# A fp32 transformer layer on one core: a reordered opening, and two modulation-row steps set between two weights

## The chip, the cores and the metric

The kernel runs on one core of a Trainium2 chip. The metric is the device time of one execution in microseconds. Engines are named as the profile names them: PE (TensorE, matrix products), PEld (its weight loads), ACT (ScalarE), DVE (VectorE), POOL (GpSimd), SP (SyncE, which issues nearly all DMA transfers; "SPq" is its queue).

## The reference

One layer on x of 512 tokens x 1024, with a conditioning vector c. All data are fp32.

```python
mod = silu(c) @ w_ada + b_ada            # 9 rows of 1024: sh1 sc1 g1 sh2 sc2 g2 sh3 sc3 g3
u = rms_norm(x, ffn1_norm_g) * (1 + sc1) + sh1
x = x + 0.5 * g1 * swiglu(u, ffn1_w_in, ffn1_w_out)     # a, b = split(u @ w_in); silu(a) * b; @ w_out
u = rms_norm(x, mix_norm_g) * (1 + sc2) + sh2
z = u @ w_mix + b_mix
...
x = x + g2 * (merged @ w_out)            # mLSTM branch and forgetting-attention branch
u = rms_norm(x, ffn2_norm_g) * (1 + sc3) + sh3
x = x + 0.5 * g3 * swiglu(u, ffn2_w_in, ffn2_w_out)
```

The change touches only the first FFN's first half, `u @ ffn1_w_in` (1024 x 5632, that is 22 pairs of 128 columns, a_j and b_j), and the rows of `mod`.

## The kernel before, in words

**Products.** An fp32 product is made of three reduced-precision ones: each operand is split into a high part (`uh`, `wh`) and a rest (`ul`, `wl`), and `mm3` (L106 to L110) adds uh by wh (L108), uh by wl (L109 or L110, as the operands are named) and ul by wh in one PSUM bank. A weight block of 128 x 1024 comes through a ring of three buffers `raw` (L76 to L80, the DMA is issued in L79 by SP), is rounded to `wh` by ACT (L89), and its rest `wl` is made by DVE (L91). A buffer of the ring comes free when its `wl` is made, or, for a piece of w_ada, when DVE has added it; SP's queue goes in order, so a load that waits for a buffer holds up every load behind it.

**The opening, `start`.** It loads x, sums its squares, makes the reciprocal roots in two chains (`chain`, on DVE), scales x by them (`norm`, L616 on ACT, one of them on DVE) and transposes the scaled x into columns (`turn`, L625, PE), four transposes for each of the eight blocks of 128 of D. The modulation of block 0, its shift and its scale, is made on PE: `mod0(v)` (L636) is eight matmuls of the pieces of w_ada with silu(c), v = 0 for the shift, v = 1 for the scale, into columns 128 to 255 and 256 to 383 of one PSUM bank, `cb` (t_207 in the rows below). For the blocks 1 to 7 DVE adds up the pieces (L641, L646, `ac`), and `sums` (L661) folds them on PE into two columns of `cb`. `u_hi` (L663 to L669, ACT) then makes the two columns `m` (L665 shift, L666 scale), `uh` and the unrounded `uf`; `u_lo` (L671, DVE) makes `ul`. Block k is 18 matmuls (L720): three products for each of six PSUM banks, the first three column pairs of the FFN. Inside block k stand the transposes for block k + 1 (at i = 7), and from k = 1 on the sums for it too (at i = 12). In block 0 those sums stand behind the 18 matmuls, behind four transposes of the identity that nobody reads (`fill(4)`, L620). All this is pinned: it is issued in the order in which it is written.

**The rest of the columns, `ffn_in`.** For j = 3 to 21: weight a_j, its 24 matmuls, a call `mid` if there is one, weight b_j, 24 matmuls, then `ffn_h` (silu on ACT L318, product `sl` on DVE L319, `hh` L320, `hl` L321), then `extra(j)`. Here `extra` makes steps of the modulation rows v = 2 to 6 (`ada_row`): step k loads a 128 x 1024 piece through the same ring `raw` and adds it up on DVE (L275 for k = 0, L277 after); step 7 also folds the sum, finishes the row with two matmuls (L289), adds the bias (L290) and stores it to `mod_d` (L291). That is 40 steps; 19 columns with two steps each make 38, and a third step is made at j = 7 and at j = 15. The accumulator `acc` and the bias row `br` share two buffers, so a row's first step waits until the row before is stored.

Of the kernel before, what the change touches and what calls it, by code (L numbers as in the profile page):

```python
# [11 lines left out]
F32 = mybir.dt.float32  # L12
F32R = mybir.dt.float32r
I32 = mybir.dt.int32
AF = mybir.ActivationFunctionType
# [5 lines left out]
P = 128  # L21
T = 512
NT = 4
# [4 lines left out]
NJ0 = 3  # L28
# [18 lines left out]
class Layer:  # L47
# [279 lines left out]
    def ffn_in(self, w_in, j0, hp, tp, extra=None, mid=None):  # L327
        for j in range(j0, NJ):
            pa, pb = self.gbank(), self.gbank()
            self.gemm_stat(pa, self.w_stat(w_in, j * P), 0, T)  # L330
            if mid:
                mid()
            self.gemm_stat(pb, self.w_stat(w_in, FF + j * P), 0, T)
            self.ffn_act(pa, pb, j, 0, T, hp, tp)
            self.lo_after = None
            if extra:
                extra(j)
# [249 lines left out]
    def start(self, st, tp):  # L587

        nc, A, sp, cp = self.nc, self.A, self.sp, self.cp
        w_in = A["ffn1_w_in"][0]  # L590
        w_ada = A["w_ada"][0]
        pin = self.tc.keep_in_program_order
# [11 lines left out]
        def chain(hf):  # L604
            v = sp.tile([P, 2], F32, name=self.nm("v"), tag="v", bufs=2)
            s2 = self.ss[:, 2 * hf:2 * hf + 2, :]
            pin(nc.vector.tensor_scalar(v, s2[:, :, 0], 1.0 / D, EPS, op0=MUL, op1=ADD))
            pin(nc.vector.scalar_tensor_tensor(v, s2[:, :, 1], 1.0 / D, v, op0=MUL, op1=ADD))
            return self.rsqrt(v, 2, pin)
        def norm(tb, h, dve=False):  # L610
            t = xn[tb, h] = st.tile([P, 512], F32, name=self.nm("xn"), tag="xs", bufs=8)
            r = rs[tb // 2][:, tb % 2:tb % 2 + 1]
            if dve:
                pin(nc.vector.tensor_scalar(t, self.x[tb][h], r, None, op0=MUL))
            else:
                pin(nc.scalar.activation(t, self.x[tb][h], AF.Copy, scale=r))  # L616
        def fill(n):

            for i in range(n):
                pin(nc.tensor.transpose(cb[:, 384:512], self.ident, self.ident))  # L620
        def turn(k, tbs):
            if k not in bt:
                bt[k] = self.tbank()
            for tb in tbs:
                pin(nc.tensor.transpose(bt[k][:, tb * P:(tb + 1) * P], xn[tb, k // 4][:, k % 4 * P:(k % 4 + 1) * P], self.ident))  # L625
        def ada_load(k):

            ars[k] = st.tile([P, NK, 2, P], F32, name=self.nm("ar"), tag="ar", bufs=7)
            halves = [(v, i) for v in range(2) for i in (0, 4)] if k == 0 else [(v, i) for i in (0, 4) for v in range(2)]
            for v, i in halves:  # L630
                nc.sync.dma_start(ars[k][:, i:i + 4, v, :], w_ada[i * P:(i + 4) * P, v * D + k * P:v * D + (k + 1) * P]
                                  .rearrange("(i p) n -> p i n", p=P))
        def mod0(v):

            for i in range(NK):
                pin(nc.tensor.matmul(cb[:, 128 * (v + 1):128 * (v + 2)], ars[0][:, i, v, :], self.ccol[:, i:i + 1].to_broadcast([P, P]),  # L636
                                     start=i == 0, stop=i == NK - 1))
# [10 lines left out]
        def load(k):  # L648
            raws[k] = self.raw(sh, [(lambda t, i=i: t[:, i, :],
                                     w_in[k * P:(k + 1) * P, i * FF:i * FF + NJ0 * P]) for i in range(2)])  # L650
# [8 lines left out]
        def sums(k):  # L659
            for v in range(2):  # L660
                pin(nc.tensor.matmul(cb[:, 2 * k + v:2 * k + v + 1], accs[k][:, v, :], self.one, start=True, stop=True))  # L661
        def u_hi(k):
            m = sp.tile([P, 2], F32, name=self.nm("m"), tag="m", bufs=4)  # L663
            c = (cb[:, 2 * k:2 * k + 1], cb[:, 2 * k + 1:2 * k + 2]) if k else (cb[:, 128:129], cb[:, 256:257])
            pin(nc.scalar.activation(m[:, 0:1], c[0], AF.Identity, bias=self.colC[:, 16 + k:17 + k]))  # L665
            pin(nc.scalar.activation(m[:, 1:2], c[1], AF.Identity, scale=self.colC[:, 8 + k:9 + k], bias=self.colC[:, 24 + k:25 + k]))  # L666
            pin(nc.scalar.activation(self.uh[k], bt[k], AF.Identity, scale=m[:, 1:2], bias=m[:, 0:1]))
            ufs[k] = self.tmp(tp, "uf")
            self.last_uf = pin(nc.scalar.activation(ufs[k], bt[k], AF.Identity, scale=m[:, 1:2], bias=m[:, 0:1]))  # L669
# [10 lines left out]
        cb = self.tbank()  # L680
# [8 lines left out]
        norm(1, 0)  # L689
        rs.append(chain(1))  # L690
        norm(2, 0, True)
        norm(3, 0)
        mod0(0)
        turn(0, (0, 1))
        turn(1, (0, 1))
        mod0(1)
        turn(0, (2, 3))
        w_hi(0)
# [9 lines left out]
        for k in range(NK):  # L708
            n = k + 1
            if k + 3 < NK:  # L710
                ada_load(k + 3)
                load(k + 3)
            wh, wl = ws[k]
            for i, (p, b) in enumerate((p, b) for p in range(3) for b in range(2 * NJ0)):
                if n < NK and i == 7:
                    turn(n, range(NT) if k else (2, 3))
                if n < NK and k and i == 12:
                    sums(n)
                s = slice(b // 2 * P, (b // 2 + 1) * P)
                pin(nc.tensor.matmul(acc_ps[b], (wl if p == 1 else wh)[:, b % 2, s], self.ul[k] if p == 2 else self.uh[k],  # L720
                                     start=k == 0 and p == 0, stop=k == NK - 1 and p == 2))
            if n < NK:
                if k == 0:
                    fill(4)
                    sums(n)
                u_hi(n)
                if k < 2:
                    norm(2 * k, 1)
                    norm(2 * k + 1, 1)
                if n + 1 < NK:  # L730
                    mod(n + 1, 1, 6)
                u_lo(n)
                if n + 1 < NK:
                    mod(n + 1, 6, 8)
                    w_hi(n + 1)
                    if n + 2 < NK:
                        mod_first(n + 2)
                    w_lo(n + 1)
# [423 lines left out]
    def run(self):  # L1162
        nc, tc, A = self.nc, self.tc, self.A
# [7 lines left out]
        with tc.tile_pool(name="f1t", bufs=1) as tp:  # L1171
            self.consts(tp)
            with tc.tile_pool(name="st", bufs=1) as st:
                acc_ps = self.start(st, tp)
            with tc.tile_pool(name="f1h", bufs=1) as hp:
                self.h_tiles(hp)
                for j in range(NJ0):
                    self.ffn_h(acc_ps[2 * j], acc_ps[2 * j + 1], j, 0, T, hp, tp)
                ada = (s for v in (2, 3, 4, 5, 6) for s in self.ada_row(v, tp, self.gbank))
                def extra(j):  # L1180
                    next(ada, None)
                    next(ada, None)
                    if j % 8 == 7:
                        next(ada, None)
                self.ffn_in(A["ffn1_w_in"][0], NJ0, hp, tp, extra)
                for _ in ada:
                    pass
                lhs = lambda k: (self.hh[k], self.hl[k])
                self.ss_tile()
                for half in range(2):  # L1190
                    bank = self.tbank if half else self.gbank
                    ada = self.ada_row(7 + half, tp, bank)
                    extra = lambda: next(ada, None)
                    self.token_gemm(lhs, NJ, A["ffn1_w_out"][0], half, self.residual(0.5, 2, half, tp), 2 + half, extra,
                                    (lambda: self.norm_half(0, tp, G2, sh2)) if half else None)
                    for _ in ada:
                        pass
                    if half == 0:
                        G2, sh2 = self.mod_cols(3, gain(R_N2))
            self.norm_half(1, tp, G2, sh2)  # L1200
            for tb in range(NT):
                for h in range(2):
                    nc.sync.dma_start(self.x_d[tb * P:(tb + 1) * P, h * 512:(h + 1) * 512], self.x[tb][h])
            for k in range(NK):
                self.dump(f"u2_{k}", self.uh[k].bitcast(F32))
# [24 lines left out]
        with tc.tile_pool(name="att", bufs=1) as ip:  # L1230
# [35 lines left out]
            for n in range(18):  # L1266
                if n % 4 == 0 and n < 16:
                    advance(fill, 99)
                    g = n // 4
                    fill = with_gates(self.fox_qkv(g + 1, ip), 4 if g else 2) if g < 3 else (s for m in range(NK) for s in self.y_a(m, yp, ip))  # L1270
# [56 lines left out]
        with tc.tile_pool(name="f2t", bufs=1) as tp, tc.tile_pool(name="f2h", bufs=1) as hp:  # L1327
# [5 lines left out]
            step = lambda *_: next(pw, None)  # L1333
# [34 lines left out]
```

## Time and profile before

| | |
|---|---|
| device time, 3 runs | 1344.37, 1344.70, 1345.14 us (median 1344.70) |
| the profiled execution's own time | 1344.62 us |
| its span | 1342.8 us |
| granted TensorE clock, mean | 1.00 |
| PE busy | 1325.6 us, 99% of the span |
| DVE / ACT / POOL busy | 66% / 44% / 3% |
| chain that ended last | PE 91%, DVE 5%, ACT 2%, DMA 1% |

The span is the time from the first to the last instruction that the profiler records; the 1.8 us between it and the execution's time lie around it and are not touched by the change. All rows below count from the span's start. A timeline row gives the start, the duration, engine, line, operation, the tile written and the tiles read, the size, the count of such instructions in a row, and in brackets the idle time before it and what ended that.

### The profile page before, as it was taken

The page shows a single profiled execution, that of the slowest core. Times are in us where ns is not written, and L with a number is a line of the kernel's source. Part 1 is how long each engine was busy: PE and PEld are TensorE (multiplying, and loading weights), DVE is VectorE, ACT ScalarE, POOL GpSimd, SP SyncE. Part 2 cuts the span into 40 slices and gives each one's busy share as a digit, 9 for nine tenths or more (in the row PEclk, how much of TensorE's full clock was granted, in tenths as well). Part 3 has the DMA queues.
Part 4 walks back from the last instruction along what each step waited for, and adds up shares of the span by engine and source line. Part 5 has one row for each costly group of instructions (what it writes and reads, how often), then busy time and mean ns, then how long its engine had stood idle before and what let it go on. Part 6 is the DMA issues. An engine that isn't in the chain of part 4 may idle for free.

```text
span 1342.8 us, 17800 instructions
## 1 busy us (share of the span) xinstructions
PE 1325.6 (99%) x6494; PEld 1110.2 (83%) x6494; DVE 888.1 (66%) x1661; ACT 590.6 (44%) x985; POOL 41.5 (3%) x66
## 2 busy tenths in 40 slices
PE   7999999999999999999999999999999999999998
PEld 6788887887889888888888888888788888888886
DVE  7865666655458758878786886446475555544777
ACT  5632333323235655556565676333253232223642
POOL 1000000000011011000000000002020000000000
PEclk9999999999999999999999999999999999999999
DMA  9766656665534344444243442364436777764574
GB/s 293 214 210 204 183 182 213 209 211 173 186 91 125 107 126 126 131 125 125 60 146 86 138 125 76 109 197 140 143 109 188 216 233 216 229 189 139 165 265 157
DMA packets 247291, 220.36 MB, mean 164 GB/s; under 512 B 13282, under 2 KB 208514, under 8 KB 247204
## 3 DMA queue, kind: packets, MB, share of 16 engines
q1 hardware_dynamic: 246820, 219.15, 53.5%
q8 instruction: 51, 0.84, 0.3%
q14 instruction: 36, 0.29, 0.1%
q0 software_dynamic: 320, 0.06, 0.0%
q10 hardware_dynamic: 64, 0.02, 0.0%
HBM read 195.00 MB, written 24.19 MB: 163 GB/s over the span
## 4 chain that ended last, share of the span: by engine, by line
PE 91%; DVE 5%; ACT 2%; DMA 1%; issue 1%; ACTq 0%; SPq 0%; DVEq 0%
PE g L110 24%; PE g L108 24%; PE g L109 24%; PE t L109 4%; PE t L110 4%; PE t L108 4%; PE g L720 2%; PE t L1094 1%; PE t L1064 1%; PE t L1035 1%; PE t L720 1%; DVE wl L91 1%; PE t L1036 1%; DMA ar<-in_w_ada_dram 1%; DVE fq L1014 1%
## 5 line engine op out<-in xcount | busy, mean ns | idle before, releaser
L89 ACT ACTIVATE wh<-raw 128x1024 fp32r<-128x1024 f32 (+2 forms) x234 | 241.3, 1036 | 421.6 <-PE g L109 145.7
L91 DVE TENSOR_TENSOR wl<-raw,wh 128x1024 fp32r<-128x1024 f32 (+2 forms) x234 | 286.4, 1226 | 184.4 <-ACT wh L89 163.7
L108 PE MATMUL g<-uh,wh 128*128 128x512 f32 (+1 forms) x976 | 367.4, 377 | 0.3 <-ACT wh L89 0.3
L110 PE MATMUL g<-uh,wl 128*128 128x512 f32 (+1 forms) x976 | 366.5, 376 | 1.2 <-DVE wl L91 1.1
L109 PE MATMUL g<-ul,wh 128*128 128x512 f32 (+1 forms) x976 | 366.5, 376 | 0.1
L110 PEld LDWEIGHTS g<-uh,wl 128*128 128x128 f32 x976 | 183.4, 188 | 35.6 <-DVE wl L91 2.1
L108 PEld LDWEIGHTS g<-uh,wh 128*128 128x128 f32 x976 | 183.5, 188 | 33.5 <-ACT wh L89 0.9
L109 PEld LDWEIGHTS g<-ul,wh 128*128 128x128 f32 x976 | 183.6, 188 | 32.8 <-POOL ul L240 0.3
L108 PE MATMUL g<-wh,uh 128*128 128x512 f32 (+2 forms) x320 | 112.4, 351 | 0.0
L110 PE MATMUL g<-wh,ul 128*128 128x512 f32 (+2 forms) x320 | 111.6, 349 | 0.0
L109 PE MATMUL g<-wl,uh 128*128 128x512 f32 (+2 forms) x320 | 111.4, 348 | 0.0
L277 DVE SCALAR_TENSOR_TENSOR acc<-raw,ccol,acc 128x1024 f32<-128x1024 f32 x49 | 62.8, 1282 | 14.1 <-DMA raw<-in_w_ada_dram 13.5
L108 PEld LDWEIGHTS g<-wh,uh 128*128 128x128 f32 x320 | 60.4, 189 | 7.8 <-DVE tk L941 0.5
L110 PEld LDWEIGHTS g<-wh,ul 128*128 128x128 f32 x320 | 60.3, 189 | 7.7
L109 PEld LDWEIGHTS g<-wl,uh 128*128 128x128 f32 x320 | 60.4, 189 | 7.3
L108 PE MATMUL g<-yh,wh 128*128 128x512 f32 x128 | 50.4, 394 | 0.0
L110 PE MATMUL g<-yh,wl 128*128 128x512 f32 x128 | 50.2, 392 | 0.0
L109 PE MATMUL g<-yl,wh 128*128 128x512 f32 x128 | 49.7, 388 | 0.0
L1046 ACT ACTIVATE S<-S,mn 128x128 f32<-128x128 f32 (+1 forms) x64 | 35.6, 556 | 16.8 <-DVE mn L1038 8.4
L109 PE MATMUL t<-wl,A 128*128 128x512 f32 x88 | 34.3, 390 | 1.1 <-DVE wl L91 1.1
L108 PE MATMUL g<-wh,hh 128*128 128x512 f32 x88 | 35.0, 398 | 0.0
L110 PE MATMUL g<-wh,hl 128*128 128x512 f32 x88 | 34.9, 396 | 0.0
(331 smaller groups left out, 2059.5 us busy)
## 6 DMA issues: line engine op xcount, KB each, us to landing
raw<-in_ffn_w_in_dram SPq DMA_DIRECT2D x82, 512.0 KB
raw<-in_w_ada_dram SPq DMA_DIRECT2D x56, 512.0 KB
raw<-in_w_mix_dram SPq DMA_DIRECT2D x46, 512.0 KB
raw<-in_ffn_w_out_dram SPq DMA_DIRECT2D x33, 512.0 KB
s<-in_ffn_w_out_dram SPq DMA_DIRECT2D x44, 256.0 KB
ws<-s SPq DMA_DIRECT2D x22, 512.0 KB
raw<-in_w_mix_dram SPq DMA_DIRECT2D x33, 256.0 KB
ar<-in_w_ada_dram SPq DMA_DIRECT2D x32, 256.0 KB
```

Of the source, the lines that this page charges most:

```text
L89: nc.scalar.activation(hi, src, AF.Copy)
L91: nc.vector.tensor_tensor(lo, src, hi, op=SUB)
L108: mm(ps, lh, rh, start=start, stop=False)
L109: mm(ps, lh, rl, start=False, stop=False)
L110: self.last_mm = mm(ps, ll, rh, start=False, stop=stop)
L277: nc.vector.scalar_tensor_tensor(acc, r, self.ccol[:, k:k + 1], acc, op0=MUL, op1=ADD)
L720: pin(nc.tensor.matmul(acc_ps[b], (wl if p == 1 else wh)[:, b % 2, s], self.ul[k] if p == 2 else self.uh[k], start=k == 0 and p == 0, stop ...
L1014: nc.vector.scalar_tensor_tensor(lo, b[own, :], gc[own, :], d[own, :], op0=MUL, op1=SUB)
L1035: nc.tensor.matmul(ps[:, :w], q[:, s], k[:, :w], start=True, stop=False)
L1036: nc.tensor.matmul(ps[:, :w], q[:, s], kl[:, :w], start=False, stop=True)
L1046: nc.scalar.activation(S[:, ws], S[:, ws], AF.Exp, scale=-1.0, bias=m, accum_out=sm[:, qb:qb + 1])
L1064: tr = lambda b, c, qb, kb: nc.tensor.transpose(b[:, c:c + P], S[:, P_OFF[qb] + kb * P:P_OFF[qb] + (kb + 1) * P], self.ident)
```

## The change

**In the opening** `mod0(0)` and the shift column `m_col(0, 0)` are written ahead of the last scaling of x, `norm(3, 0)`. So ACT makes the shift column of block 0 right after the first eight matmuls, and only the scale column stands behind the second eight. The first two transposes of block 1 move from between the two `mod0` into block 0, which now holds all four. `fill(4)` is gone. **In `ffn_in`** `mid` gets the number of the column, every `extra` makes two steps, and the two odd steps are made in `mid`, between a_j and b_j, at j = 9 and j = 15 (before: as a third step behind b_j, at j = 7 and j = 15).

```diff
--- before.py
+++ after.py
@@ -329,7 +329,7 @@
             pa, pb = self.gbank(), self.gbank()
             self.gemm_stat(pa, self.w_stat(w_in, j * P), 0, T)
             if mid:
-                mid()
+                mid(j)
             self.gemm_stat(pb, self.w_stat(w_in, FF + j * P), 0, T)
             self.ffn_act(pa, pb, j, 0, T, hp, tp)
             self.lo_after = None
@@ -659,11 +659,18 @@
         def sums(k):
             for v in range(2):
                 pin(nc.tensor.matmul(cb[:, 2 * k + v:2 * k + v + 1], accs[k][:, v, :], self.one, start=True, stop=True))
+        ms = {}
+        def m_col(k, v):
+            if v == 0:
+                ms[k] = sp.tile([P, 2], F32, name=self.nm("m"), tag="m", bufs=4)
+            c = 2 * k + v if k else 128 * (v + 1)
+            pin(nc.scalar.activation(ms[k][:, v:v + 1], cb[:, c:c + 1], AF.Identity, scale=self.colC[:, 8 + k:9 + k] if v else 1.0,
+                                     bias=self.colC[:, 16 + 8 * v + k:17 + 8 * v + k]))
         def u_hi(k):
-            m = sp.tile([P, 2], F32, name=self.nm("m"), tag="m", bufs=4)
-            c = (cb[:, 2 * k:2 * k + 1], cb[:, 2 * k + 1:2 * k + 2]) if k else (cb[:, 128:129], cb[:, 256:257])
-            pin(nc.scalar.activation(m[:, 0:1], c[0], AF.Identity, bias=self.colC[:, 16 + k:17 + k]))
-            pin(nc.scalar.activation(m[:, 1:2], c[1], AF.Identity, scale=self.colC[:, 8 + k:9 + k], bias=self.colC[:, 24 + k:25 + k]))
+            if k:
+                m_col(k, 0)
+            m_col(k, 1)
+            m = ms[k]
             pin(nc.scalar.activation(self.uh[k], bt[k], AF.Identity, scale=m[:, 1:2], bias=m[:, 0:1]))
             ufs[k] = self.tmp(tp, "uf")
             self.last_uf = pin(nc.scalar.activation(ufs[k], bt[k], AF.Identity, scale=m[:, 1:2], bias=m[:, 0:1]))
@@ -689,10 +696,10 @@
         norm(1, 0)
         rs.append(chain(1))
         norm(2, 0, True)
+        mod0(0)
+        m_col(0, 0)
         norm(3, 0)
-        mod0(0)
         turn(0, (0, 1))
-        turn(1, (0, 1))
         mod0(1)
         turn(0, (2, 3))
         w_hi(0)
@@ -713,7 +720,7 @@
             wh, wl = ws[k]
             for i, (p, b) in enumerate((p, b) for p in range(3) for b in range(2 * NJ0)):
                 if n < NK and i == 7:
-                    turn(n, range(NT) if k else (2, 3))
+                    turn(n, range(NT))
                 if n < NK and k and i == 12:
                     sums(n)
                 s = slice(b // 2 * P, (b // 2 + 1) * P)
@@ -721,7 +728,6 @@
                                      start=k == 0 and p == 0, stop=k == NK - 1 and p == 2))
             if n < NK:
                 if k == 0:
-                    fill(4)
                     sums(n)
                 u_hi(n)
                 if k < 2:
@@ -1177,14 +1183,9 @@
                 for j in range(NJ0):
                     self.ffn_h(acc_ps[2 * j], acc_ps[2 * j + 1], j, 0, T, hp, tp)
                 ada = (s for v in (2, 3, 4, 5, 6) for s in self.ada_row(v, tp, self.gbank))
-                def extra(j):
-                    next(ada, None)
-                    next(ada, None)
-                    if j % 8 == 7:
-                        next(ada, None)
-                self.ffn_in(A["ffn1_w_in"][0], NJ0, hp, tp, extra)
-                for _ in ada:
-                    pass
+
+                step = lambda: next(ada, None)
+                self.ffn_in(A["ffn1_w_in"][0], NJ0, hp, tp, lambda j: (step(), step()), lambda j: j in (9, 15) and step())
                 lhs = lambda k: (self.hh[k], self.hl[k])
                 self.ss_tile()
                 for half in range(2):
```

Three places show what moves. The first is PE in the opening (xn_266 and xn_268 are the scaled x of tokens 0 to 255, t_298 and t_301 the banks of the transposed blocks 0 and 1). Before:

```order
L636 MATMUL t_207<-ccol,ar_150 128x128 [waits DMAHW4_49]
L636 MATMUL t_207<-ccol,ar_150 128x128 x3
L625 MATMUL t_298<-ident,xn_266 128x128 [waits Activation_49]
L625 MATMUL t_298<-ident,xn_268 128x128 [waits Activation_49]
L625 MATMUL t_301<-ident,xn_266 128x128
L625 MATMUL t_301<-ident,xn_268 128x128
L636 MATMUL t_207<-ccol,ar_150 128x128 [waits DMAHW5_49]
L636 MATMUL t_207<-ccol,ar_150 128x128 x3
L636 MATMUL t_207<-ccol,ar_150 128x128 [waits DMAHW6_49]
L636 MATMUL t_207<-ccol,ar_150 128x128 x3
L625 MATMUL t_298<-ident,xn_286 128x128 [waits DVE_49]
L625 MATMUL t_298<-ident,xn_288 128x128 [waits Activation_49]
```

and with the change, where t_300 is the bank of block 0:

```order
L636 MATMUL t_207<-ccol,ar_150 128x128 [waits DMAHW4_49]
L636 MATMUL t_207<-ccol,ar_150 128x128 x3
L625 MATMUL t_300<-ident,xn_266 128x128 [waits Activation_49]
L625 MATMUL t_300<-ident,xn_268 128x128 [waits Activation_49]
L636 MATMUL t_207<-ccol,ar_150 128x128 [waits DMAHW5_49,Activation_49]
L636 MATMUL t_207<-ccol,ar_150 128x128 x3
L636 MATMUL t_207<-ccol,ar_150 128x128 [waits DMAHW6_49]
L636 MATMUL t_207<-ccol,ar_150 128x128 x3
L625 MATMUL t_300<-ident,xn_286 128x128 [waits DVE_49]
L625 MATMUL t_300<-ident,xn_298 128x128 [waits Activation_49]
```

Two transposes are gone from between the two groups of L636, and the first matmul of the second group waits for ACT as well as for its data. The second place is ACT, the same stretch. Before:

```order
L616 ACTIVATE xn_266<-x_133,rq_249 128x512 [waits DMAHW1_49,DVE_49]
L616 ACTIVATE xn_268<-x_135,rq_249 128x512 [waits DMAHW5_49]
L616 ACTIVATE xn_288<-x_139,rq_273 128x512 [waits DMAHW1_49,DVE_49]
L665 ACTIVATE m_318<-t_207,colC 128x1 [waits PE_49]
L666 ACTIVATE m_318<-t_207,colC 128x1
L667 ACTIVATE uh_185<-t_298,m_318 128x512 [waits PE_49,Activation_49]
```

and with the change (the lines of the file have moved on, L667 makes both columns, L674 is `uh`):

```order
L616 ACTIVATE xn_266<-x_133,rq_249 128x512 [waits DMAHW1_49,DVE_49]
L616 ACTIVATE xn_268<-x_135,rq_249 128x512 [waits DMAHW5_49]
L667 ACTIVATE m_296<-t_207,colC 128x1 [waits PE_49]
L616 ACTIVATE xn_298<-x_139,rq_273 128x512 [waits DMAHW1_49,DVE_49]
L667 ACTIVATE m_296<-t_207,colC 128x1 [waits PE_49]
L674 ACTIVATE uh_185<-t_300,m_296 128x512 [waits PE_49,Activation_49]
```

The first column now waits for PE ahead of the last scaling of x (xn_288 before, xn_298 now). The third place is SP's queue at j = 15, where row v = 5 begins (the loads from in_w_ada are its steps 0 to 3, `br` its bias row, those from in_ffn_w_in the weights a15, b15 and a16). Before:

```order
L79 DMA raw_1700<-in_w_ada_dram 128x1024
L79 DMA raw_1706<-in_ffn_w_in_dram 128x8x128
L79 DMA raw_1736<-in_ffn_w_in_dram 128x8x128
L273 DMA br_1699<-in_b_ada_dram 1x1024
L79 DMA raw_1771<-in_w_ada_dram 128x1024
L79 DMA raw_1774<-in_w_ada_dram 128x1024
L291 DMA mod_d<-br_1391 1x1024
L298 DMA mr_2640<-mod_d 16x128
L79 DMA raw_1777<-in_w_ada_dram 128x1024
L79 DMA raw_1782<-in_ffn_w_in_dram 128x8x128
```

and with the change:

```order
L79 DMA raw_1696<-in_w_ada_dram 128x1024
L79 DMA raw_1702<-in_ffn_w_in_dram 128x8x128
L79 DMA raw_1732<-in_w_ada_dram 128x1024
L273 DMA br_1695<-in_b_ada_dram 1x1024
L79 DMA raw_1735<-in_ffn_w_in_dram 128x8x128
L79 DMA raw_1770<-in_w_ada_dram 128x1024
L291 DMA mod_d<-br_1387 1x1024
L298 DMA mr_2636<-mod_d 16x128
L79 DMA raw_1773<-in_w_ada_dram 128x1024
L79 DMA raw_1778<-in_ffn_w_in_dram 128x8x128
```

The load of step 1 and that of b15 have changed places: step 1 takes the buffer that b15 had, and b15 the next that comes free.

## Rows read from the trace of the kernel before

**Rows 1.** The page's first part: busy time of each engine, share, instructions.

```profile
PE 1325.6 (99%) x6494; PEld 1110.2 (83%) x6494; DVE 888.1 (66%) x1661; ACT 590.6 (44%) x985; POOL 41.5 (3%) x66
```

**Rows 2.** Waits of PE: engine, line, awaited; us in total, times, longest.

```profile
PE g L110 <- DVE wl L91: 1.1, 2, 1.0
```

**Rows 3.** Timeline of PE, opening, 11 to 25 us.

```profile
11.69 2.02 PE L636 MATMUL t<-ccol,ar 128*128 128x128 f32 x16 [0.51 <-DMA ar<-in_w_ada_dram]
13.55 0.60 PE L625 MATMUL t<-ident,xn 128*128 128x128 f32 x4
13.99 1.95 PE L636 MATMUL t<-ccol,ar 128*128 128x128 f32 x16
...
17.35 1.20 PE L720 MATMUL g<-uh,wh 128*128 128x512 f32 x4 [1.19 <-ACT uh L667]
...
21.83 0.60 PE L620 MATMUL t<-ident 128*128 128x128 f32 x4
22.26 0.50 PE L661 MATMUL t<-one,ac 128*128 128x1 f32 x4
24.17 1.20 PE L720 MATMUL g<-uh,wh 128*128 128x512 f32 x4 [1.41 <-ACT uh L667]
```

**Rows 4.** Timeline of ACT, opening, 13 to 20 us.

```profile
14.11 0.72 ACT L616 ACTIVATE xn<-x,rq 128x512 f32<-128x512 f32 x1 [1.73 <-DVE rq L135]
15.98 0.26 ACT L665 ACTIVATE m<-t,colC 128x1 f32<-128x1 f32 x1 [1.14 <-PE t L636]
16.14 0.34 ACT L666 ACTIVATE m<-t,colC 128x1 f32<-128x1 f32 x1
16.52 0.78 ACT L667 ACTIVATE uh<-t,m 128x512 fp32r<-128x512 f32 x1
```

**Rows 5.** Timeline of DVE, opening: the last pieces of block 1's modulation.

```profile
19.22 2.04 DVE L646 SCALAR_TENSOR_TENSOR ac<-ar,ccol,ac 128x256 f32<-128x256 f32 x4
```

**Rows 6.** Windows, 20 to 24 us: busy of PE, PEld, DVE, ACT, POOL; PEclk, DMA share, GB/s.

```profile
20.00:24.00 4.00, 2.77 (x17) 2.29 (x15) 3.79 (x9) 1.65 (x4) 0.00 (x0) 1.00 1.17 313
```

**Rows 7.** Timeline of all engines, 202 to 206.5 us: the start of j = 16.

```profile
202.24 1.06 ACT L89 ACTIVATE wh<-raw 128x1024 fp32r<-128x1024 f32 x1 [3.99 <-DMA raw<-in_ffn_w_in_dram]
...
202.67 0.39 PE L110 MATMUL g<-uh,wl 128*128 128x512 f32 x1
203.16 0.69 DVE L319 TENSOR_TENSOR sl<-g,sl 128x512 f32<-128x512 f32 x1 [2.50 <-PE g L110]
...
203.35 0.50 PE L108 MATMUL g<-uh,wh 128*128 128x512 f32 x1 [0.30 <-ACT wh L89]
...
203.77 1.21 DVE L91 TENSOR_TENSOR wl<-raw,wh 128x1024 fp32r<-128x1024 f32 x1
...
205.04 0.50 PE L110 MATMUL g<-uh,wl 128*128 128x512 f32 x1 [0.95 <-DVE wl L91]
```

**Rows 8.** SP's queue: the loads of step 1 of row v = 5 and of a16.

```profile
186.41 0.35 SPq L79 DMA_DIRECT2D raw<-in_w_ada_dram  x1
...
197.12 0.40 SPq L79 DMA_DIRECT2D raw<-in_ffn_w_in_dram  x1
```

**Rows 9.** Timeline of DVE, 184 to 206 us: the rest of a15, the product of j = 14.

```profile
185.16 1.22 DVE L91 TENSOR_TENSOR wl<-raw,wh 128x1024 fp32r<-128x1024 f32 x1
...
191.78 0.69 DVE L319 TENSOR_TENSOR sl<-g,sl 128x512 f32<-128x512 f32 x1 [3.00 <-PE g L110]
```

**Rows 10.** A load and its rounding, of SP and ACT: a12, then b15.

```profile
151.73 0.38 SPq L79 DMA_DIRECT2D raw<-in_ffn_w_in_dram  x1
...
155.45 1.06 ACT L89 ACTIVATE wh<-raw 128x1024 fp32r<-128x1024 f32 x1 [1.22 <-DMA raw<-in_ffn_w_in_dram]
...
179.81 0.38 SPq L79 DMA_DIRECT2D raw<-in_ffn_w_in_dram  x1
...
185.34 1.06 ACT L89 ACTIVATE wh<-raw 128x1024 fp32r<-128x1024 f32 x1 [0.49 <-DMA raw<-in_ffn_w_in_dram]
```

**Rows 11.** Timeline of DVE, 99 to 101 us: the rest of b7.

```profile
99.15 1.22 DVE L91 TENSOR_TENSOR wl<-raw,wh 128x1024 fp32r<-128x1024 f32 x1
```

## The prediction, made before the changed kernel was run

> **What bounds the kernel now.** I read the busy shares first: PE works 99% of the span, no other engine over 66% except PE's own weight loads [rows 1]. So the change can win only where PE stands still or does work that nobody needs. I then read what PE waits for. On the weights' rests (L110 on `wl`) it waits twice in the whole run, 1.1 us in all, 1.0 the longest [rows 2]. The timeline then says where: the long one is at the start of j = 16, 0.95 us, with 0.30 us on `wh` just ahead of it [rows 7]. So the columns j = 8 to 10 hold next to nothing that could be won. Last I read the opening: between the matmuls of block 0 and what went before PE stands 1.19 us on `uh`, between block 0 and block 1 1.41 us; four fillers run there before the sums [rows 3].
>
> **The opening, step by step.** The first `mod0` ends at 11.69 + 2.02 = 13.71 [rows 3]. ACT, which now does nothing until 14.11, makes the shift column there: a column starts 0.04 after PE's end (15.98 against 13.99 + 1.95 = 15.94) and lasts 0.26 [rows 3, 4], so it runs from 13.75 to 14.01. It is done before the scaling of 14.11, which waits for DVE's `rq` and is not delayed. But the second `mod0` writes the bank that this column reads, and its first matmul now waits for ACT. PE starts 0.05 after ACT's end (17.35 against 16.52 + 0.78 = 17.30), that is at 14.06 instead of 13.99. A group that begins after a wait takes 2.02, not 1.95 [rows 3], so it ends at 16.08 and the scale column starts at 16.12, against 16.14 now [rows 4]: **-0.02**. The two transposes taken out (four last 13.99 - 13.55 = 0.44, two 0.22) and the shift column taken off the chain (16.14 - 15.98 = 0.16) would be worth 0.38; the wait takes almost all of it back. That the bank wait really lasts until ACT has finished no row of before shows, since nothing there writes the bank while a column is read: at one end it costs all of this, at the other nothing (-0.38). I take the first, because the changed order names ACT among the awaited; the other is a rival.
>
> The Trainium skill bears on this: PSUM — Partial Sum Buffer, section "PSUM bank collisions raise a hardware error", wants accesses guarded by bank and quadrant and not by address, since the hardware does not arbitrate. It speaks against this part: the columns are disjoint, but by that rule the wait must stand (-0.02), by addresses alone it could go (-0.38). No run here shows yet which time results.
>
> Block 0 then holds four transposes where it held two: **+0.22**. They wait for nothing new: the bank they write frees when `uf` of block 0 is done, long before the seventh matmul. The four fillers go: 22.26 - 21.83 = **-0.43** [rows 3]. The sums then start at 22.26 - 0.43 + 0.22 - 0.02 = 22.03; DVE's last piece for them is ready at 19.22 + 2.04 = 21.26 [rows 5], so nothing is late in their place. The gap of 1.41 behind them is the columns and `uh` of block 1, which are unchanged and follow the sums. The opening's sum is **-0.23**. It reaches the end only if no stall downstream is gated by something that did not move; the one large stall, at j = 16, is treated next, and the work of ACT and DVE in blocks 1 to 7 hangs on these same sums.
>
> **j = 8 to 10.** The third step no longer stands behind j = 7, so a8's load takes a buffer earlier, at the end of b7's rest, 99.15 + 1.22 = 100.37 [rows 11]; j = 9 gets its odd step in between. PE has no wait there worth naming [rows 2], DVE does the same sums: **0**. What covers it is PE's 24 matmuls per weight.
>
> **j = 15 and 16, where it costs.** Step 1's load takes b15's place and is issued at 179.81; b15's goes out when a15's rest is done, 185.16 + 1.22 = 186.38, that is at 186.41, where step 1's went [rows 8 to 10]. How long will it take? A weight load with little else in flight took 155.45 - 151.73 = 3.72 from issue to the start of its rounding; b15 of before, issued close behind a15, took 185.34 - 179.81 = 5.53 [rows 10]. I take 3.72, because in the new order no load goes out in the 6 us before b15's, and the next one waits for it; 5.53 is the other end. Then `wh` runs from 190.13 for 1.06, `wl` starts 0.04 later, 191.23, and lasts 1.22, to 192.45. On DVE the product `sl` of j = 14 is queued behind it; it started at 191.78 [rows 9]. Neighbours on DVE overlap by 0.08 (203.16 + 0.69 against 203.77 [rows 7]), so now it starts at 192.37, 0.59 late.
>
> Who waits for that? Behind `sl` on DVE stand the bias of row v = 4, its store, then step 0 of row v = 5 (which waits for the store), step 1, and a16's load waits for the buffer that step 1 frees. All are a chain without slack, so a16 is issued 0.59 late, at 197.71, not 197.12 [rows 8]. It takes 202.24 - 197.12 = 5.12 again, and `wh` runs from 202.83 to 203.89. Before, `wl` of a16 could have started at 202.24 + 1.06 + 0.04 = 203.34, and started at 203.77, because the product of j = 15 stood ahead of it [rows 7]. That is 0.43 of slack. Now it starts at 203.89 + 0.04 = 203.93, 0.16 late, and PE's wait at 205.04 ends 0.16 late: **+0.16**. Nothing else at j = 16 moves: the product of j = 15 is still ahead of `wl` and waits for PE's own last matmul of j = 15. Step 2's load, now behind b15, goes out at about 192.5 and lands before step 1 is added.
>
> **Sum.** 1344.62 (the profiled execution; the median of the runs is 1344.70, so it stands for them) - 0.23 + 0.16 = 1344.55, say **1344.6**. What can be told from no change is 0.2%, 2.7 us: the forecast is no difference. The slack makes a point of decision: b15 costs nothing up to a landing of 3.56, and eats the opening's whole gain at 3.56 + 0.23 = 3.79.
>
> **Rivals.**
> *A, the bank wait costs nothing.* The first column is read while the second group is written, or ACT is early enough: the opening gives -0.38 + 0.22 - 0.43 = -0.59, and the time is 1344.62 - 0.59 + 0.16 = 1344.2. For it: ACT is idle before 14.11 [rows 4]. Against: the changed order has the wait. Chance 0.08.
> *B, b15's load is as slow as before.* With 5.53 the chain is 5.53 - 3.72 = 1.81 later, the stall at j = 16 grows by 1.97: 1344.62 - 0.23 + 1.97 = 1346.4, a little slower. For: the transfer engines are busy with stores and step loads in these columns, and 5.12 for a16 is no outlier [rows 7, 8]. Against: nothing is issued beside it. Chance 0.10.
> *C, the stall at j = 16 goes.* This is what a step in another place could do if it freed DVE or a buffer earlier: PE would begin j = 16 at 202.67 + 0.23 and lose neither 0.30 nor 0.95 nor the slow restarts, 205.04 - 202.67 - 3 x 0.23 = 1.68 in all [rows 7]. Time 1344.62 - 0.23 - 1.68 = 1342.7. Against: `wl` of a16 stays behind the product of j = 15, which PE itself ends. Chance 0.05.
> *D, slower: without fillers PE's clock falls.* Between block 0 and block 1 PE has a gap, and the fillers stand ahead of it. If the granted clock fell to its lower level of 1.2 GHz from 2.4 GHz there, the next block, 21.83 - 17.35 = 4.48 us of work [rows 3], would take twice as long: 1344.62 + 4.48 = 1349.1. It decides if the clock falls in the 1.4 us gap. Against: it is 1.00, the higher level, over a stretch that holds the same gap [rows 6], and the gap does not grow, since the fillers are ahead of the sums and not in it. Chance 0.03.
> By the Trainium skill, TensorE: Matmul & The Clock Gate, Part 1 ("What's actually happening"), the throttled state is the default and activity releases it, so removed fillers are a risk by rule; the trace agrees only in that the clock stays at 1.00 here with them.
> That the change does nothing at all is inside the forecast.
>
> **How the numbers follow.** Forecast 0.70, A 0.08, B 0.10, C 0.05, D 0.03, unforeseen 0.04, half to each side. A, B and C lie within 2.7 us of before, so the same has 0.70 + 0.08 + 0.10 + 0.05 = 0.93; slower D and half the unforeseen, 0.05; faster the other half, 0.02. The range takes in A and B. To the fastest case (A with b15 at no cost, 1344.62 - 0.59 = 1344.0) and the slowest (B, 1346.4) I add the spread of the three runs, 0.77: 1343.3 to 1347.1. Left out are C, D and the unforeseen, 0.12.
>
> **What the changed profile would show.** Right: no L620 behind block 0; sums near 22.0; four transposes in block 0; the second L636 group near 14.06, waiting for ACT's column; first matmul of block 1 near 23.94; b15's load issued near 186.2 (all of this 0.23 earlier), `sl` of j = 14 late by some 0.6 against PE, PE waiting at j = 16 about 1.1 on `wl`. Wrong: a PEclk under 1 from 16 to 30 us (D); a wait at j = 16 of 2 us or more (B) or of none (C); the second L636 group starting at 13.77 (A); any new wait of PE at j = 8 to 10, or an opening that gives its 0.23 back in the blocks 1 to 7 because a load or a DVE piece ends the wait there and not the sums.

## The result, and the profile after

The changed kernel took **1347.76 us** (median of ten executions, 1344.77 to 1351.55), before on the same chip 1344.68 (ten, 1344.26 to 1345.76): a ratio of 1.0021, 95% interval 1.0013 to 1.003. The forecast was 1344.6, its range ended at 1347.1. Slower by 3.1 us, then, and with executions 6.8 us apart instead of 1.5.

The profile shown with it is of the fastest of the ten (1344.77 us, span 1342.9), so it holds the smaller part of the loss. The timeline of PE in the opening, as in [rows 3]:

```profile
11.04 2.02 PE L636 MATMUL t<-ccol,ar 128*128 128x128 f32 x16
12.91 0.38 PE L625 MATMUL t<-ident,xn 128*128 128x128 f32 x2
13.42 2.05 PE L636 MATMUL t<-ccol,ar 128*128 128x128 f32 x16
...
16.73 1.19 PE L727 MATMUL g<-uh,wh 128*128 128x512 f32 x4 [1.04 <-ACT uh L674]
...
18.45 0.60 PE L625 MATMUL t<-ident,xn 128*128 128x128 f32 x4
...
21.42 0.50 PE L661 MATMUL t<-one,ac 128*128 128x1 f32 x4
23.32 1.23 PE L727 MATMUL g<-uh,wh 128*128 128x512 f32 x4 [1.40 <-ACT uh L674]
```

and ACT beside it, the first column and the delayed second one (L667 both), as in [rows 4]:

```profile
13.11 0.26 ACT L667 ACTIVATE m<-t,colC 128x1 f32<-128x1 f32 x1 [1.11 <-PE t L636]
13.65 0.72 ACT L616 ACTIVATE xn<-x,rq 128x512 f32<-128x512 f32 x1 [0.28 <-DVE rq L135]
15.51 0.35 ACT L667 ACTIVATE m<-t,colC 128x1 f32<-128x1 f32 x1 [1.13 <-PE t L636]
```

The order is what the prediction said: four transposes in block 0, no fillers, the second group of L636 0.05 after ACT's column (13.11 + 0.26 = 13.37, then 13.42). From the first L636 to block 1 it takes 23.32 - 11.04 = 12.28, before 24.17 - 11.69 = 12.48 [rows 3]: -0.20.

At j = 15 and 16 more was lost than forecast. SP's queue with b15's load, then step 2's, the store of row 4 and a16's:

```profile
185.56 0.38 SPq L79 DMA_DIRECT2D raw<-in_ffn_w_in_dram  x1
...
192.18 0.33 SPq L79 DMA_DIRECT2D raw<-in_w_ada_dram  x1
193.96 0.25 SPq L291 DMA_DIRECT2D mod_d<-br  x1
...
197.92 0.40 SPq L79 DMA_DIRECT2D raw<-in_ffn_w_in_dram  x1
```

ACT's rounding of b15 and a16, which tells when they landed:

```profile
189.83 1.06 ACT L89 ACTIVATE wh<-raw 128x1024 fp32r<-128x1024 f32 x1 [3.79 <-DMA raw<-in_ffn_w_in_dram]
...
202.88 1.06 ACT L89 ACTIVATE wh<-raw 128x1024 fp32r<-128x1024 f32 x1 [5.45 <-DMA raw<-in_ffn_w_in_dram]
```

DVE: the rest of b15, the product of j = 14, step 0 of row 5, and the product of j = 15:

```profile
190.93 1.23 DVE L91 TENSOR_TENSOR wl<-raw,wh 128x1024 fp32r<-128x1024 f32 x1 [4.79 <-ACT wh L89]
192.07 0.69 DVE L319 TENSOR_TENSOR sl<-g,sl 128x512 f32<-128x512 f32 x1
...
195.82 0.75 DVE L275 TENSOR_SCALAR acc<-raw,ccol 128x1024 f32<-128x1024 f32 x1 [1.29 <-DMA mod_d<-br]
...
202.34 0.69 DVE L319 TENSOR_TENSOR sl<-g,sl 128x512 f32<-128x512 f32 x1 [1.07 <-PE g L110]
```

and PE at the start of j = 16, to be held against [rows 7]:

```profile
203.99 0.50 PE L108 MATMUL g<-uh,wh 128*128 128x512 f32 x1 [1.76 <-ACT wh L89]
...
205.25 0.50 PE L110 MATMUL g<-uh,wl 128*128 128x512 f32 x1 [0.53 <-DVE wl L91]
```

PE waits 1.76 + 0.53 = 2.29 there, before 0.30 + 0.95 = 1.25: 1.04 more, not 0.16. The longer part is now the wait on `wh`, that is on a16's landing, and no longer the one on the rest `wl`. So this execution loses 1.04 - 0.20 = 0.8 on its way to j = 16, yet is only 0.1 longer than the profiled one of before: its first L636 stood 0.65 earlier, which differs from execution to execution. The other 2 to 3 us of the median are not in this profile.

### The profile page after: what moved, and what is told of

Read it like the earlier page. It is cut to its first block, busy times and chain, and to the rows that moved or that the text cites. A ratio compares the mean times of both kernels' runs of the same rounds, so it can differ in the third digit from the quotient of the medians.

```text
span 1342.9 us, 17791 instructions
## 1 busy us (share of the span) xinstructions
PE 1324.7 (99%) x6490; PEld 1109.0 (83%) x6490; DVE 887.8 (66%) x1661; ACT 590.9 (44%) x985; POOL 41.5 (3%) x66
## 4 chain that ended last, share of the span: by engine, by line
PE 88%; DVE 6%; ACT 2%; DMA 2%; issue 1%; ACTq 0%; DVEq 0%
PE g L110 23%; PE g L108 22%; PE g L109 22%; PE t L109 4%; PE t L110 4%; PE t L108 4%; PE g L727 2%; PE t L1100 1%; DMA raw<-in_ffn_w_in_dram 1%; DVE wl L91 1%; PE t L1070 1%; PE t L1041 1%; PE t L727 1%; PE t L1042 1%; ACT wh L89 1%
```

## The experiments

Each kernel ran eleven times, unless said, with before on the same chip. Its median there was 1344.54 for the first four runs, 1344.57 for the next four, 1344.86 for the next four and 1344.61 for the last three.

In the expectations T stands for the transfers as the cause and C for the clock (rival D of the prediction). T15, T9 and C1 to C3 are finer forms of these; D2 is the longer wait at j = 16 together with a fall of the clock behind it.

**1. The changed kernel again**, unaltered.

> The changed kernel once more, unaltered, for the spread of its executions and a second profile. Its first ten executions ran from 1344.8 to 1351.6 us (before: 1344.3 to 1345.8). Theory T (transfers): the load of b15, now issued 6.6 us later and without slack, lands later in some executions than in others, and each 0.1 us of it goes to the stall at the start of j = 16; then a slower profile shows a longer wait at j = 16 (over 2.3 us in all on wh and wl) at a granted clock of 1.00 in the opening. Theory C (clock): without fillers the granted clock falls somewhere behind block 0 in some executions; then a slower profile shows a PEclk under 1.00 in some stretch, and the wait at j = 16 stays near 2.3 us. Median by both: about 1347.8.

1348.69 us (six executions, 1345.99 to 1350.72), ratio 1.0029 (1.0017 to 1.004). This time the profile was of a longer one, 1348.91. Windows of one us (columns as in [rows 6]) behind block 0:

```profile
22.00:24.00 2.00, 0.60 (x6) 0.51 (x5) 1.89 (x5) 1.53 (x4) 0.00 (x0) 1.00 1.12 335
24.00:25.00 1.00, 1.00 (x4) 0.80 (x4) 0.93 (x4) 1.00 (x3) 0.00 (x0) 0.72 1.20 296
...
26.00:27.00 1.00, 1.00 (x5) 0.73 (x4) 0.96 (x3) 0.38 (x1) 0.00 (x0) 0.50 1.20 308
27.00:28.00 1.00, 1.00 (x5) 0.90 (x4) 0.57 (x2) 0.51 (x1) 0.00 (x0) 0.58 0.98 309
28.00:29.00 1.00, 1.00 (x8) 0.83 (x7) 0.93 (x3) 0.00 (x0) 0.00 (x0) 1.00 1.02 289
```

The granted clock falls from 1.00 to 0.50 (2.4 to 1.2 GHz) right behind the gap between block 0 and block 1, and is back after some 3 us; PE is busy all the while, with 3 to 5 matmuls in a us instead of 6 to 9 in the first profile. Against before, PE is 0.36 early at the sums and 1.25 late by 54 us: 1.6 us for one fall. Theory C, rival D of the prediction with its 3 in 100, is true of this execution. The wait at j = 16 is here 1.28 + 0.53 = 1.81, at a clock of 1.00. And there is a second fall, near the end, behind a wait that no part of the change touches (before it was 1.07):

```profile
1313.69 0.50 PE L109 MATMUL t<-wl,A 128*128 128x512 f32 x1 [1.72 <-DVE wl L91]
...
1314.00:1319.00 5.00, 5.00 (x16) 3.91 (x15) 2.58 (x3) 2.21 (x3) 0.00 (x0) 0.66 0.75 227
```

PE is 2.6 late against before at the first of these rows and 4.2 at its last matmul, so 1.6 of this execution's loss belongs to neither theory. The next runs say how much belongs to the opening and how much to the rows.

**2. The opening alone**, the modulation rows of before.

> The changed opening with the modulation rows of before. T: the cost lies in the rows, so this gives 1344.7 - 0.2 = 1344.5, with executions no further apart than those of before (1.5 us). C: the cost lies in the opening, so this gives about 1347.8 with executions up to 1351.

1345.54 us (1344.72 to 1346.51), ratio 1.0006 (0.9997 to 1.0015). Between the two forecasts, T's 1344.5 and C's 1347.8: five of eleven executions have a mean clock of 0.998, the shortest of them 1345.54; no execution of before beside the runs told here was under 0.999.

**3. The rows alone**, the opening of before.

> The opening of before with the changed modulation rows. T: about 1348.0 (1347.8 + 0.2), executions several us apart. C: the profile of the changed kernel shows 1.05 us more at j = 16, so 1344.7 + 1.05 = 1345.8, executions no further apart than those of before.

1347.08 us (1345.25 to 1348.27), ratio 1.0016 (1.0007 to 1.0025). Between C's 1345.8 and T's 1348.0: the rows carry most of it, and their executions are 3 us apart. Its profile, of a 1345.90 one, has waits of 1.52 + 0.52 at j = 16.

**4. The changed kernel with its four fillers.**

> The changed kernel with the four fillers back in front of the first sums. T: 1347.8 + 0.4 = 1348.2, executions as far apart as the changed kernel's. C: the clock stays up, so about 1344.7 - 0.2 + 0.4 + 1.05 = 1346.0, executions close together.

1346.42 us (1345.42 to 1349.43), ratio 1.0016 (1.0007 to 1.0025): nearer to C's 1346.0 than to T's 1348.2, but the executions are 4 us apart, which C did not expect, and one took 1349.4 at a mean clock of 0.997. So fillers help (1348.69 without them in run 1), and there may be another fall somewhere. The profile, of a 1345.88 one, has waits of 2.01 + 0.53 at j = 16, with the clock at 1.00 behind them.

**5. Only the step of j = 15 moved**: `extra` makes the third step at j = 7, `mid` at 15.

> Before with only the step of j = 15 moved between its two weights (the step of j = 7 stays behind b7). Theory T15: the whole cost of the rows lies at j = 15, where three transfers (b15's load, the store of row 4, a16's load) now follow one another without slack: 1347.1 us, as with both steps moved, and in the profile about 2.0 us of waits at the start of j = 16. Rival T9: the step at j = 9 has a share: under 1346. What is still open in either: the profile of both steps showed only 0.74 us more at j = 16, the median 2.5 more.

1347.31 us (1345.44 to 1349.25), ratio 1.0018 (1.0008 to 1.0027): T15 holds, and this step alone costs as much as both (1347.08 in run 3). The profile is of a longer execution, 1347.75, and shows what was open. PE at j = 16:

```profile
204.97 0.50 PE L108 MATMUL g<-uh,wh 128*128 128x512 f32 x1 [1.70 <-ACT wh L89]
...
206.23 0.80 PE L110 MATMUL g<-uh,wl 128*128 128x512 f32 x1 [0.53 <-DVE wl L91]
206.83 0.63 PE L108 MATMUL g<-uh,wh 128*128 128x512 f32 x1
207.25 0.63 PE L109 MATMUL g<-ul,wh 128*128 128x512 f32 x1
```

and the windows there:

```profile
203.00:206.00 3.00, 1.00 (x4) 0.30 (x2) 1.74 (x2) 1.97 (x3) 0.00 (x0) 1.00 0.87 289
206.00:207.00 1.00, 0.77 (x2) 0.67 (x3) 1.00 (x3) 0.66 (x1) 0.00 (x0) 0.59 0.03 12
207.00:208.00 1.00, 1.00 (x4) 0.81 (x3) 1.00 (x2) 0.00 (x0) 0.00 (x0) 0.50 0.74 201
...
209.00:210.00 1.00, 1.00 (x5) 0.82 (x4) 0.55 (x2) 0.00 (x0) 0.00 (x0) 0.71 0.50 150
```

The waits are 2.23, as long as in the profile of the changed kernel, but the clock falls behind them. Matmuls then follow one another every 0.42 us instead of 0.23. PE was 0.22 late against before at 103 us, and is 2.69 late by 271: 2.47, of which the waits are 2.23 - 1.25 = 0.98, and the fall 1.5.

**6. Only the odd step of j = 7 moved**, to between a9 and b9.

> Before with only the odd step of j = 7 moved between a9 and b9. T15: no wait of PE at j = 8 to 10, so 1344.5 as before. T9: over 1345.5, with a wait of PE at j = 9 to 11 in the profile.

1344.59 us against 1344.57, ratio 1.0001 (0.9992 to 1.001). Nothing, as forecast.

**7. The changed opening with the fillers back**, rows of before.

> The changed opening with the four fillers back, rows of before. Theory C1 (the clock falls behind block 0 only without fillers): no execution at a mean clock of 0.998 or less; time 1344.5 + 0.2 = 1344.7. Rival C2 (the changed opening drops the clock anyhow): as without fillers, 1345.5, five of eleven executions at 0.998.

1344.94 us (1344.53 to 1345.47), ratio 1.0003 (0.9994 to 1.0011); all executions but one at 1.0, one at 0.999. C1 holds: without fillers the same opening ran up to 1346.5, with five of eleven at 0.998 (run 2).

**8. Before without its fillers**: the line `fill(4)` deleted, nothing else.

> Before without the four fillers, nothing else. C1: some executions at 0.998 and some 1.6 us longer than the others; median between 1344.1 (1344.5 - 0.43, no drop) and 1345.7 (a drop in all). C2: 1344.1, no execution at 0.998.

1345.35 us (1343.89 to 1346.83), ratio 1.0006 (0.9997 to 1.0015). Five executions at 0.998, all at 1345.35 or more; the two shortest took 1343.9. This is how I read the fillers: 0.43 us of PE's time in every execution, against 1.6 us in some. The interval of the median holds 1; the mean clocks say more: 0.998 in ten of the 22 executions without fillers (runs 2 and 8), in none of the 22 with fillers ahead of the gap or in it (runs 7 and 10).

**9. Third steps at j = 7 and 17**, in before: a try at a better place.

```diff
-                    if j % 8 == 7:
+                    if j in (7, 17):
```

> Before with its third steps at j = 7 and 17 in place of 7 and 15. The load of step 3 no longer stands ahead of a16's, so a16 is issued when step 0 is added (195.8, not 197.1), lands by about 200.9, and its rest is made ahead of the product of j = 15 on DVE. If the wait at j = 16 is what limits there, it goes: 1344.55 - 1.7 = 1342.9, and no wait over 0.3 at j = 16. Rival: the third step at j = 17 makes a wait of its own: 1344.5, with a wait at j = 17 or 18.

**1343.20 us** (1342.58 to 1343.70), ratio 0.9987 (0.9978 to 0.9996). The wait of PE at j = 16 is gone, and none stands at j = 17 or 18; SP and DVE show why. The queue, a16 and b16, then the next step's load:

```profile
195.22 1.72 SPq L79 DMA_DIRECT2D raw<-in_ffn_w_in_dram  x2
197.86 0.35 SPq L79 DMA_DIRECT2D raw<-in_w_ada_dram  x1
```

DVE, the rest of a16 ahead of the product of j = 15:

```profile
200.16 1.23 DVE L91 TENSOR_TENSOR wl<-raw,wh 128x1024 fp32r<-128x1024 f32 x1 [2.33 <-ACT wh L89]
202.52 0.69 DVE L319 TENSOR_TENSOR sl<-g,sl 128x512 f32<-128x512 f32 x1 [1.13 <-PE g L110]
```

With one load less in the queue a16 goes out 1.9 earlier than before (195.22 against 197.12 [rows 8]; the execution itself is 0.6 ahead there), and its rest is ready before PE asks.

**10. Six fillers in the gap**, behind the sums and behind ACT's two columns, in before, and none ahead of the sums.

```diff
                 if k == 0:
-                    fill(4)
                     sums(n)
                 u_hi(n)
+                if k == 0:
+                    fill(6)
```

> Before with six fillers behind the sums and ACT's two columns, inside the gap in which PE waits for uh of block 1, in place of four ahead of the sums. They need 0.66 us of the about 0.8 that ACT needs for uh, so they delay nothing: 1344.55 - 0.43 = 1344.1. Theory C1 (a gap of 1.4 us without work drops the clock when too little stood ahead of it): work in the gap holds the clock, no execution at 0.998 or less, executions within 1.5 us. Rival C3 (only work ahead of the sums counts, or the clock is down to chance): some at 0.998, median 1345.3 as with the fillers just left out.

1344.18 us (1343.56 to 1345.30) against 1344.86, ratio 0.9996 (0.9987 to 1.0005); no execution under 0.999. As C1 had it, though the 0.4 us alone is within what the interval can tell.

**11. Both, 9 and 10.**

> The fillers in the gap and the third steps at 7 and 17 together. If both hold, 1344.55 - 0.43 - 1.7 = 1342.4; faster than before and than the changed kernel.

**1342.83 us** (1341.83 to 1343.15), ratio 0.9984 (0.9975 to 0.9993): faster than both kernels. The fillers run while ACT makes `uh`, and the next block does not wait for them: it starts 1.91 behind the sums (23.73 - 21.82), as before (24.17 - 22.26).

```profile
21.82 0.50 PE L661 MATMUL t<-one,ac 128*128 128x1 f32 x4
22.92 0.88 PE L620 MATMUL t<-ident 128*128 128x128 f32 x6 [0.59 <-ACT m L666]
23.73 0.96 PE L720 MATMUL g<-uh,wh 128*128 128x512 f32 x3
```

**12. The step of j = 15 moved, and PE kept at work in the wait** by twelve transposes behind b15's last matmul.

> The step of j = 15 between its two weights, as in the run with that alone (1347.3, executions from 1345.4 to 1349.3, four of eleven at a mean clock of 0.998 or less), with twelve transposes of the identity, 1.3 us, behind the last matmul of j = 15, where PE waits about 2.2 us anyhow. Theory D2 (the wait at j = 16 costs twice: itself, about 0.9 us more than before, and the clock that falls behind it): the clock stays up, no execution at 0.998 or less, median 1345.5 to 1345.8. Rival T (transfers alone, of varying length, make up the 2.7 us): 1347.3 as without.

1347.35 us (1346.94 to 1349.98), ratio 1.0021 (1.0012 to 1.003), which looks like T. But the second FFN's `ffn_in` has a `mid` too, so the twelve also stood in its j = 15, where PE has nothing to wait for and its next matmul starts 1.23 later for them:

```profile
1170.09 1.47 PE L337 MATMUL g<-ident 128*128 128x128 f32 x12
1171.32 0.47 PE L108 MATMUL g<-uh,wh 128*128 128x512 f32 x1
```

So the median can't decide. The profile, of the longest execution (1349.98), shows something else: in the first FFN the twelve ended at 204.08, PE then waited 1.52 + 0.52, and the clock fell all the same:

```profile
205.60 0.50 PE L108 MATMUL g<-uh,wh 128*128 128x512 f32 x1 [1.52 <-ACT wh L89]
...
207.00:208.00 1.00, 1.00 (x3) 0.81 (x4) 1.00 (x2) 0.23 (x1) 0.00 (x0) 0.50 0.24 45
```

Work put into this wait does not hold the clock in every execution.

**13. The same in the first FFN alone.**

```diff
             self.gemm_stat(pb, self.w_stat(w_in, FF + j * P), 0, T)
+            if j0 == NJ0 and j == 15:
+                b = self.gbank()
+                for i in range(12):
+                    self.tc.keep_in_program_order(self.nc.tensor.transpose(b[:, 0:P], self.ident, self.ident))
```

> As the run with the filled wait, but the twelve transposes behind j = 15 of the first FFN alone. Theory D2 (wait plus fallen clock): 1345.5 to 1346.0, most executions at a mean clock of 0.999 or 1.0. Rival T (transfers alone): 1347.3, as without fillers.

1345.86 us (1345.32 to 1347.45), ratio 1.0011 (1.0002 to 1.002). This is D2's forecast. It agrees with run 12: with the 1.23 of the second FFN, and the 0.25 by which before was longer there, it makes 1347.34, against 1347.35. One execution still has 0.998, the 1347.45. In the profile the transposes end before the weight is there and delay nothing; behind them PE waits 0.83 + 0.52, and the clock from 206 to 210 us is at 1.00:

```profile
202.52 1.47 PE L337 MATMUL g<-ident 128*128 128x128 f32 x12
204.83 0.50 PE L108 MATMUL g<-uh,wh 128*128 128x512 f32 x1 [0.83 <-ACT wh L89]
...
206.09 0.50 PE L110 MATMUL g<-uh,wl 128*128 128x512 f32 x1 [0.52 <-DVE wl L91]
```

**14. Run 5 once more**, beside it on the same chip.

> The step of j = 15 between its weights, without fillers, a second time: 1347.3 by both theories, executions from 1345.4 to 1349.3. D2: those at 0.998 or less are the longer ones, by about 1.6 us.

1347.30 us (1344.81 to 1348.26), ratio 1.0016 (1.0007 to 1.0025), 1.44 over run 13, whose interval overlaps with this one. The profile, of a 1348.26 one, has waits of 3.13 + 0.52 at j = 16 and the clock at 0.50 behind them:

```profile
205.57 0.50 PE L108 MATMUL g<-uh,wh 128*128 128x512 f32 x1 [3.13 <-ACT wh L89]
...
207.00:208.00 1.00, 1.00 (x3) 0.81 (x4) 1.00 (x2) 0.25 (x1) 0.00 (x0) 0.50 0.32 49
```

Of what this execution lost, the longer wait is 3.65 - 1.25 = 2.40, more than the fall: the wait itself differs from execution to execution, as T had it. The mean clock reads 0.999 all the same: one fall of 3 us is 0.0012 of the span, so the mean tells a fall only together with a low tail. The second half of what D2 expected, that those at 0.998 are the longer ones, fails for that reason: the two at 0.998 took 1347.33 and 1347.38, and three at 0.999 took more.

**15. The changed kernel with the clock held in both places**, six fillers in the gap and twelve transposes at j = 15.

> The whole changed kernel with six fillers in the gap behind block 0's sums and twelve transposes in the wait at j = 16. D2 (the clock's two falls are what the prediction missed): 1344.55 - 0.2 (opening) + 1.0 (the longer wait at j = 16) = 1345.3 to 1345.6, no execution over 1347. T: 1347 or more, as the changed kernel.

1345.89 us (1344.49 to 1348.04), ratio 1.001 (1.0001 to 1.0019), a little over the forecast of 1345.3 to 1345.6, and one execution, of 1348.04, over the 1347 that none was to pass.

## Why the prediction was wrong

**Right: the opening's order and its -0.23.** The bank wait eats the early column: the second L636 group starts 0.05 behind ACT, as worked out, and the profile gives -0.20. The Trainium skill's rule (PSUM — Partial Sum Buffer, "PSUM bank collisions raise a hardware error"), guard by bank, is what the changed order does, and the trace agrees: 13.37 to 13.42. Rival A falls with it. **Right:** nothing at j = 8 to 10 (run 6).

**Mis-sized: the chain at j = 15, +0.16 for +1.04.** Two terms. b15's load, "I take 3.72", took 189.83 - 185.56 = 4.27, and 3.87 to 4.76 in the eight other profiles with this order: between the two ends, 3.72 and 5.53, and in all nine beyond the point of decision of 3.79 that the sum itself gave. And a term was left out: step 2's load now goes out behind b15, at 192.18 instead of 188.85, and is still moving when row 4 is stored. Of before, the store, step 0 that waits for it, and the window between them (DMA share 0.01); then that window with the change (0.44):

```profile
193.69 0.25 SPq L291 DMA_DIRECT2D mod_d<-br  x1
195.01 0.75 DVE L275 TENSOR_SCALAR acc<-raw,ccol 128x1024 f32<-128x1024 f32 x1 [0.76 <-DMA mod_d<-br]
193.69:195.01 1.32, 1.32 (x8) 1.09 (x7) 0.57 (x1) 0.00 (x0) 0.00 (x0) 1.00 0.01 3
...
193.96:195.82 1.86, 1.86 (x10) 1.55 (x9) 0.57 (x1) 0.00 (x0) 0.00 (x0) 1.00 0.44 178
```

From the store's issue to step 0 it took 195.82 - 193.96 = 1.86, before 195.01 - 193.69 = 1.32; in the eight others 1.49 to 1.99, and 1.32 to 1.34 in the profiles with b15 in its old place. That the load beside it slows the store is read from this comparison; no run moved that load alone. I asked only whether it lands in time, not beside what it moves. The two terms make up the miss: to the 0.59 of the prediction come 4.27 - 3.72 = 0.55 and 1.86 - 1.32 = 0.54; less the slack of 0.43, and less 0.16 because a16 took 4.96 and not 5.12, that is 1.09, for 1.04 measured. Rival B was the nearer in kind, and the sign set for it came (a wait of 2 us or more), though not its 5.53. With the clock at 1.00 in all but a few executions, this costs 1345.86 - 1344.61 = 1.25 (run 13).

**Wrong: that the clock does not fall, rival D at 0.03.** The step that failed is the argument "the gap does not grow, since the fillers are ahead of the sums and not in it". The gap is unchanged, 1.40, and the clock falls behind it all the same in part of the executions once the work ahead of it is taken away (runs 1, 2, 8), and, by the mean clocks, in none of 22 when six transposes are put into the gap itself (10, 11). My other argument, a clock of 1.00 over the stretch of [rows 6], could not tell either way: the gap ends at 24.17, those rows at 24.00, and the same window in run 1 also has 1.00, with the fall at 24.4. Of before, the window behind the gap does have 1.00,

```profile
24.00:28.00 4.00, 3.83 (x21) 3.27 (x22) 3.65 (x7) 3.26 (x6) 0.00 (x0) 1.00 1.15 308
```

but that speaks for the kernel with fillers, not for the one without. My price, a whole block at half speed, was too high: a fall costs 1.6 us.

**Not thought of: the same fall behind the longer wait at j = 16.** I priced a wait of PE at its own length. Behind the 1.25 of before its one profile shows no fall; behind longer ones some executions lose 1.5 on top (profile of run 5; 1.44 in the median between runs 14 and 13). Length alone does not decide: with 2.29 (the changed kernel's first profile), 1.52 + 0.52 (run 3) and 2.01 + 0.53 (run 4) the clock stayed.

**The account.** -0.2 for the opening, about +1.2 for the wait at j = 16, +1.4 for the clock behind it (14 against 13), and for the clock without fillers about +1.2 (run 8: +0.78 where -0.43 was due) make 3.6; the changed kernel showed +3.1 in its first ten executions and +4.2 in the next six. These are medians of different runs, and that they add up is an assumption. Holding the clock in both places leaves 1345.89 - 1344.61 = 1.3 of it (run 15). How often the clock falls behind either place in one execution was seen only in profiles, one fall in the opening (run 1) and three at j = 16 (runs 5, 12 and 14); the rest is inferred from medians. The effect of the fillers in the opening is within the interval of each single run (2, 8, 10); it rests on the profile of run 1 and on the mean clocks of runs 2, 7, 8 and 10. The share of the clock at j = 16 is less sure: the falls are in the profiles, but 1.44 between two medians is within what the two intervals leave open, the waits themselves run from 1.81 to 3.65 in the six profiles without the twelve transposes, and these did not hold the clock in run 12. The fall near the end of run 1's execution is in no term.

## What to carry to other kernels

Work that nobody reads can be load-bearing where PE pauses next to it: before deleting fillers ahead of a gap, try moving them into the gap, where the next block started no later for them (run 11). Price a wait of PE that grows at its length and, besides, at the 1.5 us that a fall of the clock behind it costs in some executions (seen here behind waits of 2.04 to 3.65 us at j = 16, and of 1.40 and 1.72 elsewhere). And when a load is moved behind another in a queue, ask what it now moves beside: here a store of 4 KB (1 x 1024 fp32) for which the next row's first step, and through it the next weight's load, were waiting, and it took some 0.5 us longer.

## What was not expected of the hardware

The granted clock fell for about 3 us at a time, to exactly 0.50, in some executions of one and the same program and not in others, behind block 0 after a gap that was the same to 0.01 us (1.40 and 1.41). By the Trainium skill, TensorE: Matmul & The Clock Gate, Part 1 ("What's actually happening"), the watch on PE's activity runs freely and is not reset when a kernel starts, so that the point of change varies from run to run. That falls come in some executions and not in others fits that; no run here shows the watch itself. In run 1 the clock also fell near the end (0.66 in the mean from 1314 to 1319 us), behind a wait of 1.72 us that no part of the change touches; behind 1.62 us in the same place it stayed (run 10). What decides, in a given execution, stays open.
